# Where the operands of the projections lie: slots of 768 columns for tokens 258 to 1025, slots of 272 for the first 258

## The chip, the cores and the metric

The kernel runs on one core of one Trainium2 chip. A core has five engines that run side by side: TensorE (PE in the profile, with PEld for its weight loads) multiplies matrices, VectorE (DVE) and ScalarE (ACT) work elementwise, GpSimd (POOL) does a few of the subtractions here, and SyncE (SP) issues most of the DMAs. They share one on-chip memory of 128 partitions; matmul results go to eight banks of a second memory (PSUM), from which ACT and DVE take them away. The metric is the device time of one launch in microseconds (us); lower is better.

## The reference

One decoder layer in float32 over 16 meta tokens and 1024 tokens, model width 1024. The part that matters here:

```python
z = h @ w_in + b_in
q, k, v, c_in, gates = split(z)
a = swa_sink_attention(q, k, v, attn_sinks, rel_bias)      # 512 wide
y_attn = a @ w_attn_proj                                   # 512 -> 1024
c = c_val * sigmoid(c_gate)
c = causal_dwconv(c, conv_dw, conv_dw_b)                   # 31 taps
c = silu(layer_norm(c, conv_ln_g, conv_ln_b))              # 512 wide
y_conv = c @ w_conv_proj                                   # 512 -> 1024
mixed = sigmoid(g_attn) * y_attn + sigmoid(g_conv) * y_conv
h = layer_norm(alpha * h + mixed @ w_out, ln1_g, ln1_b)
```

A feed-forward network with a three-tap convolution follows (up, gelu, down) and a last layer norm. The output leaves out the meta tokens.

## The kernel before, in words

**Arithmetic.** Every float32 operand of a large product is split in two parts, hi (the value rounded to the matmul's float32r type) and lo (the rest). A product is three matmuls: weight hi by moving hi, weight hi by moving lo, weight lo by moving hi. `product` (lines 301, 305, 306) issues these three for each chunk of 128 of the contraction; the weights are the stationary operand (128 columns), the moving operand holds up to 512 tokens.

**Stages.** Layer norm and q, k, v come first; then attention runs beside the gate tiles (`ps_z`, 16 tiles of three column groups, 386, 384 and 256), which fill PE while ACT and DVE work on attention and on the depthwise convolution. While the last gate tiles run, DVE and ACT normalise the convolution (`cln_centre`, `cln_var`, `cln_rstd`, `cln_scale`, `cln_split`) and scale and split the attention output (`o_split`); means and variances come from small matmuls with a matrix of ones (`mean_mms`, lines 891 and 892, tile `ps_m`). Then come the projections (`ps_p`), the product with `w_out` (`ps_w`), FFN up (line 1497) and down (line 1635).

**Layout of the moving operands of the projections.** `OA` holds attention, `OC` the convolution, each [128, 8320] float32r: eight slots (four chunks of 128 channels, hi and lo of each) of T = 1040 columns, of which the last 1026 are tokens. `oo` and `conv` return the columns a to b of a slot.

**Groups of tokens.** `UG` cuts the 1026 tokens for the norm and the attention split: 386, 384, 256. `PG` cuts them for the projections: 258, 256, 256, 256.

**The projections.** The loop runs over eight tiles m of 128 output channels. `weights` loads the 128 columns of both projection matrices, [128, 8, 128], and splits them on ACT (cast to `whi`) and DVE or POOL (`wlo`, line 276). `whi` and `wlo` alternate between two buffers each; a `wlo` buffer is 64 columns longer than 1024, and `shift` says at which column of it the weights begin (16). Each m makes, for each of the four groups, 12 matmuls on `OA` and 12 on `OC`: 192 matmuls of 258 columns and 576 of 256 in all. `merge` multiplies the sums by the gates on DVE (lines 1097 to 1107).

**Order.** The tile framework's scheduler orders each engine's instructions by ranks and its own estimate of time; DVE's norm instructions are chained in the written order (`pin`). On each engine the instructions then run strictly in that order. The order of ACT in the norm's stretch, where evacuations of gate groups (line 676), casts of weights (273), squares, reciprocal roots (959) and swishes (971) alternate, is the scheduler's. A change of function on ACT costs a table load.

**Placement.** The pools give fixed addresses, the same before and after the change: `whi` at bytes 12224 and 16320 of a partition, `wlo` at 20416 and 24768, `OA` at 136896, `OC` at 196032.

Of the kernel before, what the change touches and what calls it, by code (L numbers as in the profile page):

```python
# [24 lines left out]
R = mybir.dt.float32r  # L25
# [4 lines left out]
P = 128  # L30
D = 1024
KC = D // P
NMETA = 16
S = 1024
T = S + NMETA
U0 = 14
# [16 lines left out]
ZG = [(0, 400), (400, 784), (784, 1040)]  # L53

HG = [(0, 272), (272, 656), (656, 1040)]
UG = [(0, 386), (386, 770), (770, 1026)]

PG = [(0, 258), (258, 514), (514, 770), (770, 1026)]

# [42 lines left out]
def tile_hybrid_layer(  # L102
# [9 lines left out]
    def load(o, i):  # L112
        return nc.sync.dma_start(out=o, in_=i)
# [5 lines left out]
    def f32(ap):  # L119
        return ap.bitcast(F)  # L120
# [6 lines left out]
    @contextmanager  # L127
    def rank(p):

        saved = tc.cur_priority  # L130
        tc.cur_priority = p
        yield
        tc.cur_priority = saved
# [34 lines left out]
    sp = start.enter_context(tc.tile_pool(name="start", bufs=1, side="right", reuse_waits="tile"))  # L168
# [93 lines left out]
    def wsp(name, tag):  # L262
        return wsp_p.tile([P, D + (64 if tag == "wlo" else 0)], R, name=name, tag=tag)

    def pair_of(hi, lo, shift=0, shape=None):
        hi, lo = wsp(hi, "whi"), wsp(lo, "wlo")[:, shift:shift + D]
        return [t.rearrange("p (k c) -> p k c", k=KC) for t in (hi, lo)] if shape else [hi, lo]

    def wraw(shape):
        return wraw_p.tile(shape, F, name="wr", tag="wr")  # L270

    def split(raw, hi, lo, quick=False, behind=None):
        ins = nc.scalar.copy(hi, raw)  # L273
        if behind is not None:
            after(ins, behind)
        return (nc.vector if quick else nc.gpsimd).tensor_tensor(lo, raw, f32(hi), OP.subtract)  # L276
# [1 line left out]
    fills = [0]  # L278
    last_fill, last_split = [], []

    def weights(shape, fill):
        fills[0] += 1
        n = fills[0]
        own = n == 3
        raw = sp.tile(shape, F, name="wr3") if own else wraw(shape)
        with rank({1: 13, 2: 18, 3: 17, 4: 23}.get(n, RK_SPLIT)):
            last_fill.append(fill(raw))
        hi, lo = (sp.tile(shape, R, name=t + "3") for t in ("whi", "wlo")) if own else pair_of("whi", "wlo", 16, shape)
        if n <= 3:
            return hi, lo, raw  # L290
        with rank(RK_SPLIT):
            last_split.append(split(raw, hi, lo, n <= 23))
        return hi, lo
# [3 lines left out]
    def product(ps, terms, behind=None):  # L297

        n = len(terms)
        for i, (ah, al, bh, bl) in enumerate(terms):  # L300
            ins = nc.tensor.matmul(ps, ah, bh, start=i == 0, stop=False)  # L301
            chunks_done.append(ins)
            if i == 0 and behind is not None:
                after(ins, behind)
            nc.tensor.matmul(ps, ah, bl, start=False, stop=False)  # L305
            last = nc.tensor.matmul(ps, al, bh, start=False, stop=i == n - 1)  # L306
        return last
# [404 lines left out]
    for q4 in range(2):  # L712
        ps = pat.tile([P, 512], F, name="ps_v4", tag="t", bufs=2)
        for i in range(4):
            c = NMETA + (q4 * 4 + i) * P
            nc.tensor.transpose(ps[:, i * P:(i + 1) * P], vT[:, c:c + P], ident)
        src = ps[:, :].rearrange("p (n g d) -> p n g d", g=2, d=HD)
        for g in range(NKV):
            hi, lo = (V[:, q4 * 4:q4 * 4 + 4, g, i] for i in range(2))
# [30 lines left out]
    for h in range(NH):  # L750
        g, r = divmod(h, 4)
        o = ps[:2, h * 16:(h + 1) * 16]
# [144 lines left out]
    with rank(RK_EVAC):  # L897
        nc.scalar.copy(c_hi[:, :U], csum)
        pinned.append(nc.vector.tensor_tensor(c_lo, csum, f32(c_hi[:, :U]), OP.subtract))
        for g, (a, b) in enumerate(UG):  # L900
            means[g] = pat.tile([P, 512], F, name="ps_m", tag="st"[g % 2], bufs=2)
# [7 lines left out]
    OC = late.tile([P, 8320], R, name="OC")  # L909
# [4 lines left out]
    OA = oa_p.tile([P, 8320], R, name="OA")  # L914
# [3 lines left out]
    def temp(n):  # L918
        return tmp_p.tile([P, 386], F, name="t", tag="t", bufs=6)[:, :n]


    def conv(c, hl, a, b):
        o = (c * 2 + hl) * T + U0
        return OC[:, o + a:o + b]

    def pin(ins):

# [7 lines left out]
    def cln_centre(g):  # L935
        a, b = UG[g]
        for c in range(CH):
            pin(dve.tensor_tensor(acc[c][:, a:b], acc[c][:, a:b], means[g][:, :b - a], OP.subtract))

    def cln_var(g):  # L940
        a, b = UG[g]
        n = b - a
        s_ = temp(n)
        nc.scalar.activation(s_, acc[0][:, a:b], AF.Square)
        for c in range(1, CH):
            q_ = temp(n)
            nc.scalar.activation(q_, acc[c][:, a:b], AF.Square)
            pin(dve.tensor_tensor(s_, s_, q_, OP.add))

        hi, lo = (conv(1, hl, a, b) for hl in range(2))  # L950
        pin(dve.tensor_copy(hi, s_))
        pin(dve.tensor_tensor(lo, s_, f32(hi), OP.subtract))
        sums[g] = pat.tile([P, 512], F, name="ps_m", tag="s", bufs=2)
        mean_mms(sums[g][:, :n], ones_r, hi, lo)

    def cln_rstd(g):
        n = UG[g][1] - UG[g][0]
        pv_, r_, t_ = sums[g][:, :n], temp(n), temp(n)
        nc.scalar.activation(r_, pv_, AF.Abs_reciprocal_sqrt, bias=eps, scale=1.0)
        pin(dve.scalar_tensor_tensor(t_, pv_, EPS, r_, OP.add, OP.mult))  # L960
        pin(dve.tensor_tensor(t_, t_, r_, OP.mult))
        pin(dve.tensor_scalar(t_, t_, -0.5, 1.5, OP.mult, OP.add))
        pin(dve.tensor_tensor(r_, r_, t_, OP.mult))
        rstd[g] = r_

    def cln_scale(g):
        a, b = UG[g]
        for c in range(CH):
            y = acc[c][:, a:b]
            pin(dve.tensor_tensor(y, y, rstd[g], OP.mult))  # L970
            nc.scalar.activation(y, y, AF.Silu, bias=clnb(c), scale=clng(c))

    def cln_split(g):
        a, b = UG[g]
        for c in range(CH):
            y = acc[c][:, a:b]
            pin(dve.tensor_copy(conv(c, 0, a, b), y))
            pin(dve.tensor_tensor(conv(c, 1, a, b), y, f32(conv(c, 0, a, b)), OP.subtract))


    def oo(r, hl, a, b):
        o = (r * 2 + hl) * T + U0
        return OA[:, o + a:o + b]

    def o_split(g, r):
        a, b = UG[g]
# [89 lines left out]
    tc.cur_priority = RK_PROJ  # L1076
    early = []
    for m in range(KC):
        hi, lo = weights([P, KC, P], lambda raw: load(raw, w_ab[m]))

        def branch(i, g, tag, bufs):
            a, b = PG[g]
            ps = pat.tile([P, 512], F, name="ps_p", tag=tag, bufs=bufs)
            rhs = (oo, conv)[i]
            product(ps[:, :b - a], [(hi[:, 4 * i + k], lo[:, 4 * i + k], rhs(k, 0, a, b), rhs(k, 1, a, b))
                                    for k in range(4)])
            return ps[:, :b - a]

        def merge(g, psa, psb):
            a, b = PG[g]  # L1090
            n = b - a
            with rank(RK_EVAC):
                t = gslot()[:, :, :n]
                ins = load(t, dram(sgd, m * P * U + a, [[U, P], [KC * P * U, 2], [1, n]]))

                ta, tb = t[:, 0], t[:, 1]
                nc.vector.scalar_tensor_tensor(ta, ta, 1.0, psa, OP.add, OP.mult)
                nc.vector.scalar_tensor_tensor(tb, tb, 1.0, psb, OP.add, OP.mult)
                nc.vector.tensor_tensor(ta, ta, tb, OP.add)
                if g == 0:  # L1100
                    nc.scalar.mul(pair[:, m, 0:2], ta[:, 0:2], 0.5)
                    nc.vector.scalar_tensor_tensor(pair[:, m, 2:4], ta[:, 0:2], 0.5, f32(pair[:, m, 0:2]),
                                                   OP.mult, OP.subtract)
                v = ta[:, n - 256:].rearrange("p (t x) -> p t x", t=2)
                h = mixed2(g, m, 0)
                last_act = nc.scalar.mul(h, v, 0.5)
                nc.vector.scalar_tensor_tensor(mixed2(g, m, 1), v, 0.5, f32(h), OP.mult, OP.subtract)
            return ins, last_act

        if m < KC - 1:  # L1110
            for g in range(4):
                last_gate, last_act = merge(g, branch(0, g, "mm", 3), branch(1, g, "t", 2))
        else:
            pa = [branch(0, g, "mm", 3) if g < 3 else branch(0, g, "s", 2) for g in range(4)]
            for g in range(4):
                last_gate, last_act = merge(g, pa[g], branch(1, g, "t", 2))
        if m in (2, 3):
            raw = (FA[:, 4112:5136], OB[:, 3072:4096])[m - 2]
            load(raw, w_out_v[m + 2])
            prep_wo(m + 2, raw, last_act)  # L1120
        if m < 4:
            early.append(FA[:, W_AT[m]:W_AT[m] + 1024])
            after(load(early[m], w_out_v[m]), last_gate)
# [349 lines left out]
    for c in range(FC):  # L1473
        V4, X, Z, Y = (pup.tile([P, 1024], F, name=n, tag=n) for n in ("pw", "px", "pz", "py"))
        passes = ((1,), (0,)) if c == 0 else ((0, 1),)
        for subs in passes:
            last = subs == passes[-1]
            w_next = iter(range(7))
            a, b = SUB[subs[0]][0], SUB[subs[-1]][1]
            i = max(a, 2)  # L1480
# [309 lines left out]
```

## Time and profile before

| | |
|---|---|
| median of 3 runs | 1259.55 us (1259.47 to 1259.66) |
| the profiled execution | 1259.33 us, of which the span of its instructions is 1257.1 us |
| PE busy | 1246.0 us (99%) |
| weight loads busy | 1179.2 us (94%) |
| DVE busy | 1086.6 us (86%) |
| ACT busy | 587.4 us (47%) |
| projections (first to last `ps_p`) | 416.48 to 512.07 us of the span |
| FFN up | about 609 to 1040 us |

How to read the rows: a row of the timeline holds the start (us from the span's start), the time of the instruction or of the merged group, the engine, the line, the operation, output tile <- input tiles, the shape and the count; in brackets idle time before it and what ended it. Matmuls overlap in the pipeline, so a matmul's own time is longer than the distance between two starts. PEclk is the clock that the throttle granted, in tenths.

### The profile page before, as it was taken

To read this page: it belongs to the slowest core of one execution; us is meant where nothing else is said; L and a number is where in the kernel's file an instruction comes from. 1 tells how busy PE (TensorE), PEld (TensorE's weight loads), DVE (VectorE), ACT (ScalarE), POOL (GpSimd) and SP (SyncE) were. 2 spreads that over 40 slices of the span, in tenths; PEclk is the share of its full clock that TensorE was granted. 3 is DMA by queue.
4 is the path that set the end of the run, shared out by engine and by line. 5 is a ranking of instruction groups with operands and counts; after the bars stand their busy time and mean duration, and the time that the engine had idled before them with its cause. 6 is when DMAs were issued, how large, how long until landed. Compare 5 with 4: busy or idle time off the path is not lost.

```text
span 1257.1 us, 21713 instructions
## 1 busy us (share of the span) xinstructions
PE 1246.0 (99%) x8546; PEld 1179.2 (94%) x8546; DVE 1086.6 (86%) x1859; ACT 587.4 (47%) x1057; POOL 54.1 (4%) x28
## 2 busy tenths in 40 slices
PE   9999999999999999999999999999999999999997
PEld 8999999999999999788899999999999998888886
DVE  7899989999989587648899999999999986995697
ACT  7522244545474222335565555554555554544330
POOL 0000000010112132000000000000000000000000
PEclk9999999999999999999999999999999999999999
DMA  7294733332155565222145555463464568998722
GB/s 279 73 309 104 192 95 97 106 94 81 68 141 178 155 171 140 77 75 101 68 134 185 193 210 187 184 218 117 154 230 164 203 211 318 390 328 298 249 86 84
DMA packets 96152, 212.10 MB, mean 169 GB/s; under 512 B 10787, under 2 KB 35939, under 8 KB 95922
## 3 DMA queue, kind: packets, MB, share of 16 engines
q1 hardware_dynamic: 84282, 199.64, 47.4%
q10 hardware_dynamic: 11768, 11.08, 2.7%
q8 instruction: 67, 1.10, 0.4%
q14 instruction: 35, 0.29, 0.1%
HBM read 150.29 MB, written 62.70 MB: 169 GB/s over the span
## 4 chain that ended last, share of the span: by engine, by line
PE 96%; ACT 1%; DVE 1%; DMA 0%; issue 0%; ACTq 0%; DVEq 0%; SPq 0%
PE px L1497 14%; PE py L1497 9%; PE ps_x L1635 9%; PE ps_z L305 8%; PE ps_z L301 8%; PE ps_z L306 8%; PE ps_z L1635 7%; PE pz L1497 5%; PE pw L1497 5%; PE ps_p L306 2%; PE ps_p L301 2%; PE ps_p L305 2%; PE ps_w L306 2%; PE ps_w L301 2%; PE ps_w L305 2%; PE ps_z L517 2%
## 5 line engine op out<-in xcount | busy, mean ns | idle before, releaser
L669 DVE SCALAR_TENSOR_TENSOR FA<-cin,cols,FA 128x1026 f32<-128x1026 f32 x120 | 155.2, 1305 | 0.2
L301 PE MATMUL ps_z<-RHO,whi 128*128 128x384 f32 (+2 forms) x324 | 104.7, 323 | 0.2 <-ACT FA L676 0.2
L305 PE MATMUL ps_z<-RHC,whi 128*128 128x384 f32 (+2 forms) x324 | 104.5, 323 | 0.0
L305 PE MATMUL ps_z<-RHO,whi 128*128 128x384 f32 (+2 forms) x324 | 104.0, 321 | 0.0
L306 PE MATMUL ps_z<-RHC,wlo 128*128 128x384 f32 (+2 forms) x324 | 103.7, 320 | 0.0
L301 PE MATMUL ps_z<-RHC,whi 128*128 128x384 f32 (+2 forms) x324 | 103.7, 320 | 0.0
L306 PE MATMUL ps_z<-RHO,wlo 128*128 128x384 f32 (+2 forms) x324 | 103.4, 319 | 0.0
L1316 DVE TENSOR_TENSOR RHO<-wr,RHO 128x512 fp32r<-128x512 f32 x94 | 63.6, 686 | 5.4 <-ACT RHO L1315 5.4
L1315 ACT CAST RHO<-wr 128x512 fp32r<-128x512 f32 x94 | 56.7, 620 | 24.4 <-DVE wr L1333 11.5
L273 ACT CAST whi<-wr 128x1024 fp32r<-128x1024 f32 x37 | 38.9, 1051 | 56.3 <-PE ps_z L305 31.9
L301 PEld LDWEIGHTS ps_z<-RHO,whi 128*128 128x128 f32 x324 | 60.9, 188 | 0.9 <-ACT FA L676 0.4
L305 PEld LDWEIGHTS ps_z<-RHC,whi 128*128 128x128 f32 x324 | 60.9, 188 | 0.4
L306 PEld LDWEIGHTS ps_z<-RHC,wlo 128*128 128x128 f32 x324 | 60.9, 188 | 0.2
L301 PEld LDWEIGHTS ps_z<-RHC,whi 128*128 128x128 f32 x324 | 60.9, 188 | 0.2
L306 PEld LDWEIGHTS ps_z<-RHO,wlo 128*128 128x128 f32 x324 | 61.0, 188 | 0.1
L305 PEld LDWEIGHTS ps_z<-RHO,whi 128*128 128x128 f32 x324 | 60.9, 188 | 0.1
L1333 DVE TENSOR_TENSOR wr<-wr 128x512 f32<-128x512 f32 x88 | 60.3, 685 | 0.2
L276 POOL TENSOR_TENSOR wlo<-wr,whi 128x1024 fp32r<-128x1024 f32 x17 | 42.3, 2488 | 185.3 <-ACT whi L273 175.7
L676 ACT ACTIVATE FA<-ps_z,cols 128x386 f32<-128x386 f32 (+2 forms) x48 | 26.0, 541 | 46.6 <-PE ps_z L306 39.1
L1509 ACT COPY FA<-px 128x514 f32<-128x514 f32 (+2 forms) x23 | 13.1, 571 | 68.0 <-PE px L1497 67.8
L1316 DVE TENSOR_TENSOR ws<-wr,ws 128x512 fp32r<-128x512 f32 x60 | 40.6, 686 | 4.5 <-ACT ws L1315 4.3
L1422 ACT ACTIVATE FA<-OB,cols 128x512 f32<-128x512 f32 x44 | 35.9, 816 | 14.0 <-DVE OB L1505 14.0
(467 smaller groups left out, 3567.3 us busy)
## 6 DMA issues: line engine op xcount, KB each, us to landing
wr<-in_w_up_dram SPq DMA_DIRECT2D x44, 512.0 KB, 4.6
wr<-in_w_z_dram SPq DMA_DIRECT2D x30, 512.0 KB, 4.0
fd<-FA SPq DMA_DIRECT2D x44, 256.0 KB, 2.5
OB<-in_w_down_dram SPq DMA_DIRECT2D x19, 512.0 KB, 6.2
qt<-qd SPq DMA_DIRECT2D x28, 256.0 KB, 3.7
td<-OB SPq DMA_DIRECT2D x12, 512.0 KB
sums<-fd SPq DMA_DIRECT2D x12, 512.0 KB, 4.8
sd<-sums SPq DMA_DIRECT2D x12, 512.0 KB, 2.7
```

The source lines that it names most:

```text
L273: ins = nc.scalar.copy(hi, raw)
L276: return (nc.vector if quick else nc.gpsimd).tensor_tensor(lo, raw, f32(hi), OP.subtract)
L301: ins = nc.tensor.matmul(ps, ah, bh, start=i == 0, stop=False)
L305: nc.tensor.matmul(ps, ah, bl, start=False, stop=False)
L306: last = nc.tensor.matmul(ps, al, bh, start=False, stop=i == n - 1)
L669: nc.vector.scalar_tensor_tensor(acc[c], cin[:, j:j + U], wc, acc[c], OP.mult, OP.add)
L1315: nc.scalar.copy(hi, src)
L1316: ins = nc.vector.tensor_tensor(lo, src, f32(hi), OP.subtract)
L1333: ins = nc.vector.tensor_tensor(*x)
L1422: nc.scalar.activation(t, cc[:, 2:HW], AF.Identity, bias=ffw(3, o), scale=ffw(2, o))
L1497: ins = nc.tensor.matmul(o, x[:, ks], bmat(sub, q, hl, k), start=first and k + j == 0, stop=k == 3 and j == 2, skip_group_check=not first)
L1635: nc.tensor.matmul(banks[i], l[:, ts], r[:, ws], start=first and a and x + k == 0, stop=z and x == len(ops) - 1 and k == 2, skip_group_che ...
```

## The change

The slots change their places: the first 258 tokens of each of the eight slots lie apart, in pieces of 272 columns at the beginning (slots 0 to 2) and at the end (slots 3 to 7) of `OA` and `OC`; the other 768 tokens of each slot lie in pieces of 768 columns between them. `UG` becomes 258, 384, 384, so that no group crosses the cut. The low weights of the projections begin at column 0 of their buffer instead of 16; other weights keep 16. Every matmul keeps its shape except the twelve for the means and variances of the norm. By the scheduler, some instructions on ACT and PE stand elsewhere around the norm and at the end of the projections.

```diff
-UG = [(0, 386), (386, 770), (770, 1026)]
+UG = [(0, 258), (258, 642), (642, 1026)]
...
-    def weights(shape, fill):
+    def weights(shape, fill, shift=16):
...
-        hi, lo = (sp.tile(shape, R, name=t + "3") for t in ("whi", "wlo")) if own else pair_of("whi", "wlo", 16, shape)
+        hi, lo = (sp.tile(shape, R, name=t + "3") for t in ("whi", "wlo")) if own else pair_of("whi", "wlo", shift, shape)
...
+    def place(i, a, b):
+
+        if a < 258:
+            o = i * 272 + (6144 if i > 2 else 0)
+        else:
+            o = 816 + i * 768 - 258
+        return slice(o + a, o + b)
+
     def conv(c, hl, a, b):
-        o = (c * 2 + hl) * T + U0
-        return OC[:, o + a:o + b]
+        return OC[:, place(c * 2 + hl, a, b)]
...
     def oo(r, hl, a, b):
-        o = (r * 2 + hl) * T + U0
-        return OA[:, o + a:o + b]
+        return OA[:, place(r * 2 + hl, a, b)]
...
-        hi, lo = weights([P, KC, P], lambda raw: load(raw, w_ab[m]))
+        hi, lo = weights([P, KC, P], lambda raw: load(raw, w_ab[m]), 0)
```

## The prediction

> **What bounds the kernel.** I read the page first (span, busy shares, the chain), then the stage of the projections by itself, then single starts on TensorE (PE).
>
> ```profile
> span 1257.1 us, 21713 instructions
> PE 1246.0 (99%) x8546; PEld 1179.2 (94%) x8546; DVE 1086.6 (86%) x1859; ACT 587.4 (47%) x1057; POOL 54.1 (4%) x28
> PEclk9999999999999999999999999999999999999999
> PE 96%; ACT 1%; DVE 1%; DMA 0%; issue 0%; ACTq 0%; DVEq 0%; SPq 0%
> ```
>
> PE is busy 99% of the span at full clock, and 96% of the chain that ended last is PE. So a nanosecond between two matmul starts is a nanosecond of the kernel, and work on the other engines counts only where it makes PE wait. The change touches the stage of the projections (tile `ps_p`). Its window, for the matmuls of that tile alone (columns: stretch, its length, then busy time and count on PE, on the weight loads and on DVE, clock, DMA):
>
> ```profile
> 416.48:512.07 95.59, 90.99 (x768) 90.94 (x768) 26.44 (x63) 1.00 0.48 134
> ```
>
> 768 matmuls in 90.99 us are 118.5 ns each. The timeline shows their starts (first column, us). One output tile is two runs of 12 with 258 columns and then six runs of 12 with 256:
>
> ```profile
> 439.20 0.28 PE L301 MATMUL ps_p<-OA,whi 128*128 128x258 f32 x1
> ...
> 442.07 0.28 PE L301 MATMUL ps_p<-OA,whi 128*128 128x256 f32 x1
> ...
> 450.55 0.28 PE L301 MATMUL ps_p<-OA,whi 128*128 128x258 f32 x1
> ```
>
> 24 matmuls of 258 columns take 442.07 - 439.20 = 2.87 us, 119.6 ns each; 72 of 256 take 8.48 us, 117.8 ns each. The third number of a row (0.28) is the modelled end of one matmul and not the spacing. Eight tiles of this make 8 x 11.35 = 90.8 us, the 90.99 of the window. Now the same shape in the next stage, FFN up (L1497), where a row holds a whole run of 12:
>
> ```profile
> 690.17 1.60 PE L1497 MATMUL px<-RHC,RHO 128*128 128x258 f32 x12
> 691.61 1.52 PE L1497 MATMUL px<-OC,RHO 128*128 128x256 f32 x12
> ...
> 702.78 1.52 PE L1497 MATMUL py<-OC,RHO 128*128 128x256 f32 x12
> 704.14 1.52 PE L1497 MATMUL px<-OA,RHO 128*128 128x256 f32 x12
> 705.50 1.52 PE L1497 MATMUL px<-RHC,RHO 128*128 128x256 f32 x12
> 706.86 1.52 PE L1497 MATMUL py<-OA,ws 128*128 128x256 f32 x12
> 708.22 1.52 PE L1497 MATMUL py<-RHC,ws 128*128 128x256 f32 x12
> 709.58 0.28 PE L1497 MATMUL px<-RHC,ws 128*128 128x258 f32 x1
> ```
>
> From 702.78 to 709.58 are 60 matmuls of 256 columns in 6.80 us: 113.3 ns, 4.5 ns under the projections, same clock, same order (high part twice, low part once). The run of 258 at 690.17 takes 1.44 us, 120.0 ns: two columns more cannot cost 6.7 ns where 256 cost 113.3 (0.44 each, so 0.9).
>
> **The distances.** What differs is where the operands lie. The pools put `whi` at bytes 12224 and 16320 of a partition, `wlo` at 20416 and 24768, `OA` at 136896 and `OC` at 196032: each leaves 192 when divided by 256. A chunk of weights is 512 bytes, which keeps the remainder. Before, a slot of the projections is 1040 columns, 4160 = 16 x 256 + 64 bytes, so from slot to slot the remainder moves on by 64, and `wlo` begins 16 columns later, at remainder 0. In up, the runs of 256 columns begin at column 48 or 2048 n + 48 of `OC`, `OA` or `RHC`, remainder 128, and step by 1024 bytes; their weights, hi and lo, are all at remainder 192: one distance, 113.3 ns. The runs of 258 step by 1032 bytes, so their distances wander: 120.0 ns. The modulus 256 is my reading of these runs; no row prints an address.
>
> After, tokens from 258 on lie in slots of 768 columns, 3072 = 12 x 256 bytes, beginning 816 columns into `OA` and `OC`: remainder 192 + 3264, that is 128. With shift 0 `wlo` is at 192 like `whi`. Every moving slice then lies 64 bytes from its weights, as in up's runs of 256: the three groups of 256 get the operand distance of the rows of 113.3 ns.
>
> **The sum, part by part.**
> 1. 576 matmuls of 256 columns (8 tiles x 72): from 117.8 to 113.4 (113.3 in the rows; I leave 0.1 for the joints with runs at other distances): -2.5 us, all on PE with nothing beside it. Bounds: 0 if the distance is not the cause, -2.6 at 113.3.
> 2. 192 matmuls of 258 columns (first tokens, slots of 272 columns, 1088 = 4 x 256 + 64 bytes): the distance still steps by 64. Lower bound, all at the good distance: 113.3 + 0.9 = 114.2, -1.0 us; upper bound the wandering 120.0 of row 690.17, +0.1, for the range +0.3, since no run shows these very steps. I take +0.1, the end nearest to what the slots still do.
> 3. Split by 258/384/384: as many instructions on ACT and DVE as before and 1026 columns in both; the mean and variance matmuls (L891, L892) likewise. Nothing on a queue of SP or POOL is added; two loads on SP change places.
> 4. The order on ACT moves, and there is one PE wait:
>
> ```profile
> 382.08 0.28 PE L306 MATMUL ps_z<-RHC,wlo 128*128 128x256 f32 x1
> 382.56 0.44 PE L301 MATMUL ps_z<-RHO,whi 128*128 128x386 f32 x1 [0.21 <-ACT FA L676]
> 382.84 0.34 PE L305 MATMUL ps_z<-RHO,whi 128*128 128x386 f32 x1
> 383.02 0.33 PE L306 MATMUL ps_z<-RHO,wlo 128*128 128x386 f32 x1
> ```
>
> ```profile
> 375.00 1.06 ACT L273 CAST whi<-wr 128x1024 fp32r<-128x1024 f32 x1 [0.76 <-ACT FA L676]
> 375.97 0.46 ACT L676 ACTIVATE FA<-ps_z,cols 128x256 f32<-128x256 f32 x1
> 376.45 1.28 ACT L959 ACT_TABLE_LOAD   x1
> 376.46 0.33 ACTq L117 DMA_DIRECT2D sgd<-FA  x1
> 377.74 0.47 ACT L959 ACTIVATE t<-ps_m,eps 128x256 f32<-128x256 f32 x1
> 378.23 1.28 ACT L971 ACT_TABLE_LOAD   x1
> 379.53 2.51 ACT L971 ACTIVATE FA<-FA,cols 128x384 f32<-128x384 f32 x4
> 381.94 0.56 ACT L676 ACTIVATE FA<-ps_z,cols 128x386 f32<-128x386 f32 x1
> ```
>
> PE starts a gate group at 382.56, 0.48 after the matmul before it instead of 0.12, and the next start is 0.28 later instead of 0.18: 0.46 us lost. The bank it wants is emptied by the ACT evacuation at 381.94. Behind the cast of 375.00 stand, before it, an evacuation, a table load, a reciprocal root, a table load and four swishes: 5.9 us from the cast's end. In the changed order the last reciprocal root stands ahead of the cast, and behind the cast come one table load (1.28), four swishes (2.51), one evacuation (0.46) and an issue (0.33), 4.6 us. With the cast's end no later than 376.0 the bank is free by 381.2, a microsecond before PE wants it (382.2). I take the whole wait out: -0.45; bounds -0.46 and +0.3 (the cast late by another table load and a root, 1.75: the bank is free at 382.95, and the wait grows to 0.75).
> 5. The third column group of the projections (514 to 770) now needs the last part of attention, which it did not need before:
>
> ```profile
> 411.99 0.43 DVE L991 TENSOR_TENSOR OA<-OB,OA 128x256 fp32r<-128x256 f32 x1
> ...
> 422.19 0.28 PE L301 MATMUL ps_p<-OA,whi 128*128 128x256 f32 x1
> ```
>
> DVE is done at 412.42 and that group begins at 422.19: 9.8 us of cover, so 0. If it were gone, each microsecond DVE is later is one of PE.
>
> Sum: -2.5 + 0.1 - 0.45 = -2.85. Behind the stage PE is the chain, and the engines that follow it start earlier by as much. The profiled execution took 1259.33 us (2.2 more than its span), 0.2 under the median 1259.55 of the runs: 1256.5 against it, 1256.7 against the median.
>
> **A rule that speaks against it.** The rows have one shape at 117.8 and at 113.3 ns. The Trainium skill, "TensorE: Matmul & The Clock Gate", Back-to-back issue gap, gives the warm gap of a single matmul by its column count alone (an estimate by it for 256 columns: 109.2 ns), and its Part 2 says that loading the next weights "doesn't steal SBUF read bandwidth from the running matmul". By that rule the addresses cannot matter and part 1 would be 0 instead of -2.5; this trace does not agree with one gap per shape.
>
> **Rivals.**
> - The distance is not the cause, and 4.5 ns belong to something else of the stage, for instance its three source lines or the writes of the merges beside it. Then only the wait goes: 1259.55 - 0.45 = 1259.1. For it: no row prints an address. Against it: up has both figures, 113.3 and 120.0, in one stage and from one line. Chance 0.12. The page's rule above would give this time.
> - The matmuls gain but the wait of 0.46 stays, moves or doubles, since ACT's order is another: 1259.55 - 2.4 = 1257.15, up to 1257.5 with +0.3. Chance 0.20.
> - Slower: PE is held in the norm itself. PE reaches the variance matmul of the first group one gate group earlier than now.
>
> ```profile
> 357.00 0.56 DVE L952 TENSOR_TENSOR OC<-t,OC 128x386 fp32r<-128x386 f32 x1
> ...
> 358.92 4.00 DVE L948 TENSOR_TENSOR t<-t 128x384 f32<-128x384 f32 x3
> ```
>
> ```profile
> 359.74 0.34 PE L891 MATMUL ps_m<-OC,ones_r 128*128 128x386 f32 x1
> ```
>
>   DVE has its operand at 357.56, 2.2 us before PE takes it. With 258 columns instead of 386 DVE gets there about 1.2 us earlier (an estimate: nine instructions, 0.56 for 386 in row 357.00 and 0.43 for 256 in row 411.99), and PE by the 12 matmuls of 256 that now stand behind, 1.4; some 2.0 are left. Row 358.92 shows three instructions in 4.00 us which take 1.9 undisturbed: 2.1 lost once. One such loss ahead of the matmul costs PE 0.1 us; three (6.3 - 2.0 = 4.3) outweigh the gain: 1259.55 - 2.85 + 4.3 = 1261.0. It decides from 4.9 us of delay on; the trace has one loss there. Chance 0.07.
>
> **How the numbers follow.** The likeliest case, 0.61, gives 1256.7, with a range of its own from 1255.6 (part 2 at -1.0) to 1257.3 (the wait half kept, part 2 at +0.3). The second rival reaches 1257.5 and the first 1259.1; to leave no more than 2 in 10 out the range goes from 1255.6 to 1258.4, where half a gain of part 1 would also lie. 0.2% is 2.5 us, about what a measurement of this kernel tells from no change: faster than 1257.03 means most of the likeliest case and a little of the second, 0.57; within 0.2% are the rest of these and the first rival, 0.36; slower 0.07.
>
> **What would show it.** Part 1: runs of 12 of 256 columns in `ps_p` take 1.36 us instead of 1.41. Part 2: those of 258 stay near 1.43. Part 4: no start on PE is marked as released by ACT L676 near 382. Part 5: no gap in PE at the third group of the first tile. The prediction is wrong if the runs of 256 stay at 1.41, or if a PE gap over 1 us stands between 355 and 425.

## The result, and the profile after

The changed kernel takes 1257.75 us (median of 22 runs, 1257.42 to 1258.00) against 1259.41 (22 runs) for the kernel before: ratio 0.9986, 95% interval 0.9980 to 0.9991. It is faster by 1.66 us, 0.13%: a real difference, since the interval lies below 1, but within the 0.2% that the forecast set as a bound, the outcome to which it gave 0.36. The forecast was 1256.7, 2.85 us less, with a range from 1255.6 to 1258.4; the time lies inside it, and the size was too large by 1.2 us. The profiled execution took 1257.53 us, 2.1 more than its span.

The page of the changed kernel (span, busy time of each engine, and the chain that ended last):

```profile
span 1255.4 us, 21714 instructions
PE 1244.7 (99%) x8546; PEld 1178.1 (94%) x8546; DVE 1086.2 (87%) x1859; ACT 586.4 (47%) x1057; POOL 54.0 (4%) x28
...
PE 97%; DVE 1%; ACT 1%; DMA 0%; issue 0%; SPq 0%; DVEq 0%
```

PE is still the whole chain. The span is 1.7 us shorter, and PE has 1.3 us less to do. In the window of the projections (stretch, length, then busy time and count on PE, on the weight loads and on DVE, clock, DMA) the same 768 matmuls take 89.90 instead of 90.99 us, at the same granted clock (summed from start to start it is 1.25 us less; the busy time also counts the modelled end of the last matmul of a stretch, and the changed kernel has one stretch more):

```profile
416.27:510.17 93.90, 89.90 (x768) 89.84 (x768) 26.44 (x63) 1.00 0.50 141
```

The starts on PE (timeline of the changed kernel) show where. A tile is 24 matmuls of 258 columns and 72 of 256; rows with 258 on `OA` begin a tile, the others are starts of runs of 12:

```profile
419.17 0.29 PE L301 MATMUL ps_p<-OA,whi 128*128 128x256 f32 x1
...
420.55 0.28 PE L301 MATMUL ps_p<-OC,whi 128*128 128x256 f32 x1
...
421.91 0.28 PE L301 MATMUL ps_p<-OA,whi 128*128 128x256 f32 x1
...
427.35 0.28 PE L301 MATMUL ps_p<-OA,whi 128*128 128x258 f32 x1
...
430.24 0.28 PE L301 MATMUL ps_p<-OA,whi 128*128 128x256 f32 x1
...
438.72 0.28 PE L301 MATMUL ps_p<-OA,whi 128*128 128x258 f32 x1
...
441.62 0.29 PE L301 MATMUL ps_p<-OA,whi 128*128 128x256 f32 x1
...
449.79 0.28 PE L301 MATMUL ps_p<-OA,whi 128*128 128x258 f32 x1
```

The tiles take turns. In tiles 0 and 2 the 72 matmuls of 256 columns take 427.35 - 419.17 = 8.18 and 449.79 - 441.62 = 8.17 us, with runs of 12 at 1.36 (420.55 to 421.91): 113.3 ns a matmul, as forecast. In tile 1 they take 438.72 - 430.24 = 8.48 us, 117.8 ns, as before the change. This goes on to the end: tiles 0, 2, 4 and 6 are short, 1, 3 and 5 long. The last tile, which has its own order, has both:

```profile
496.13 0.29 PE L301 MATMUL ps_p<-OA,whi 128*128 128x256 f32 x1
...
500.22 0.28 PE L301 MATMUL ps_p<-OC,whi 128*128 128x258 f32 x1
...
501.66 0.29 PE L301 MATMUL ps_p<-OC,whi 128*128 128x256 f32 x1
...
503.03 0.39 PE L301 MATMUL ps_w<-RX,RHC 128*128 128x512 f32 x1
...
508.77 0.28 PE L301 MATMUL ps_p<-OC,whi 128*128 128x256 f32 x1
...
510.18 0.39 PE L306 MATMUL ps_w<-OA,RHC 128*128 128x512 f32 x1
```

Its 36 on `OA` take 500.22 - 496.13 = 4.09 us, 113.6 each; its first 12 on `OC` take 1.37; then come matmuls of the next product, and the last run of 12 on `OC` takes 510.18 - 508.77 = 1.41 again. So one and the same set of weights and slots runs at both spacings.

The account in the profiled executions: the 576 matmuls of 256 columns take 1.42 us less (four tiles at 0.31, the last one 0.18), the 192 of 258 take 0.17 more (441.62 - 438.72 = 2.90 and 430.24 - 427.35 = 2.89 us for 24, against 2.87). The wait of PE at 382 is gone, which the first experiment shows, and the stage begins 0.21 us earlier (416.27 against 416.48). Both together are 1.46. Of the remaining 0.2 of the span, most lies in a wait at the beginning of FFN up. The rows before and after it, first of the kernel before, then of the changed one:

```profile
618.42 1.58 PE L1497 MATMUL px<-RHC,ws 128*128 128x256 f32 x12
619.83 1.58 PE L1497 MATMUL py<-RHC,ws 128*128 128x256 f32 x12
621.72 0.99 PE L1497 MATMUL px<-RHC,RHO 128*128 128x258 f32 x6 [0.31 <-ACT OB L1509]
```

```profile
616.92 1.52 PE L1503 MATMUL px<-RHC,ws 128*128 128x256 f32 x12
618.28 1.59 PE L1503 MATMUL py<-RHC,ws 128*128 128x256 f32 x12
619.98 1.69 PE L1503 MATMUL px<-RHC,RHO 128*128 128x258 f32 x12
```

From the start of the last run of 256 to the next are 1.89 us before and 1.70 after. This pause differs from kernel to kernel (in the runs below 0.30 to 0.91 us lie between the last start ahead of it and the first behind it), so a difference of some tenths between two kernels can come from there.

The rows ahead of the pause show something that the forecast overlooked. The run at 618.42 takes 619.83 - 618.42 = 1.41 us before, and the same run takes 618.28 - 616.92 = 1.36 us after, though the change touches neither the shapes nor the addresses of this stage. In the kernel before, five of the first seven runs of 256 in FFN up (609.05 to 619.83) take 1.41 to 1.42 us; the other two have a wait in or behind them, and every run from 629.24 on takes 1.36. So the stage that served as the model had both spacings, at one distance, before anything was changed.

**Two theories** stood after this. A, the buffer: `whi` and `wlo` alternate between two buffers, and the remainders of `wlo` by 512 differ (448 and 192), so that the weights of even tiles suit the slots and those of odd tiles do not. B, the state: at these distances two spacings hold themselves, 113.3 and 117.8 ns, and what ran just before (the 24 matmuls of 258 columns, whose distances still wander) sets the one or the other. The last tile speaks against A, but its order is its own.

### The profile page after: what moved, and what is told of

Read it like the earlier page. It is cut to its first block, busy times and chain, and to the rows that moved or that the text cites. A ratio compares the mean times of both kernels' runs of the same rounds, so it can differ in the third digit from the quotient of the medians.

```text
span 1255.4 us, 21714 instructions
## 1 busy us (share of the span) xinstructions
PE 1244.7 (99%) x8546; PEld 1178.1 (94%) x8546; DVE 1086.2 (87%) x1859; ACT 586.4 (47%) x1057; POOL 54.0 (4%) x28
## 4 chain that ended last, share of the span: by engine, by line
PE 97%; DVE 1%; ACT 1%; DMA 0%; issue 0%; SPq 0%; DVEq 0%
PE px L1503 15%; PE py L1503 9%; PE ps_x L1641 9%; PE ps_z L305 8%; PE ps_z L301 8%; PE ps_z L306 8%; PE ps_z L1641 7%; PE pz L1503 5%; PE pw L1503 5%; PE ps_p L301 2%; PE ps_p L306 2%; PE ps_p L305 2%; PE ps_w L306 2%; PE ps_w L301 2%; PE ps_w L305 2%; PE ps_z L517 2%
```

## The experiments

### The split of norm and attention alone

```diff
 (the kernel before)
-UG = [(0, 386), (386, 770), (770, 1026)]
+UG = [(0, 258), (258, 642), (642, 1026)]
```

> The kernel before with the split of norm and attention by 258, 384 and 384 tokens alone; slots and distances stay. Both theories on the spacing expect all runs of 12 matmuls of 256 columns at 1.41 us and those of 258 near 1.43. If the change's norm part is what took the wait of 0.46 us at 382 away, the wait is gone here too, the projections begin some 0.2 us earlier (as after the change) and the time is 0.2 to 0.5 us under before. If the wait went for another reason (the new places of the slots moved the scheduler's order), it stands here and the time is that of before.

Measured: 1259.32 us against 1259.65, ratio 0.9997 (0.9988 to 1.0007), which does not tell it from no change. Runs of 256 columns stay at 1.41 us. The wait is gone, by the same order on ACT as in the changed kernel (ACT's timeline of this kernel):

```profile
374.26 0.58 ACT L959 ACTIVATE t<-ps_m,eps 128x384 f32<-128x384 f32 x1
374.74 1.04 ACT L273 CAST whi<-wr 128x1024 fp32r<-128x1024 f32 x1
...
379.86 0.57 ACT L676 ACTIVATE FA<-ps_z,cols 128x386 f32<-128x386 f32 x1
```

The last reciprocal root stands ahead of the cast, the bank is empty at 380.43, and PE goes on without a pause. So the split alone takes the wait away. But the projections begin at 416.42, only 0.06 us earlier than before and not the expected 0.2. A gate matmul that starts at 342.06 in the kernel before, ahead of the norm, already starts 0.16 later in this one (342.21); the way from it to the projections is 0.22 shorter (74.20 instead of 74.42). That is still less than the wait was worth, and the rest is lost next to the wait; the rows are those of the kernel before and then of the changed one, which does the same:

```profile
342.06 0.42 PE L305 MATMUL ps_z<-RHC,whi 128*128 128x384 f32 x1
```

```profile
342.14 0.42 PE L305 MATMUL ps_z<-RHC,whi 128*128 128x384 f32 x1
...
382.24 0.28 PE L306 MATMUL ps_z<-RHC,wlo 128*128 128x256 f32 x1
382.35 0.34 PE L301 MATMUL ps_z<-RHO,whi 128*128 128x386 f32 x1
382.53 0.34 PE L305 MATMUL ps_z<-RHO,whi 128*128 128x386 f32 x1
```

From the row at 342 to the first matmul of the projections are 416.48 - 342.06 = 74.42 us before and 416.27 - 342.14 = 74.13 after: 0.29 less, where the wait was worth 0.47 (0.48 + 0.28 became 0.11 + 0.18). The other 0.18 goes back into the matmuls beside it: the stretch to the matmul ahead of the wait takes 40.10 instead of 40.02 us, and the rest of the way another 0.1. From start to start most of it, 0.13, lies in the 146 gate matmuls of 384 columns on this way (25.61 us instead of 25.48). The gate matmuls have the same shapes and addresses as before, but the small matmuls for the variance (258 and 384 columns instead of 386, 384 and 256) stand elsewhere among them. That these shift the spacing of their neighbours is argued from theory B, not shown. The figure is steady: in the twelve other kernels here the same way takes 74.13 to 74.20.

### Two distances again

```diff
 (the changed kernel)
-        hi, lo = weights([P, KC, P], lambda raw: load(raw, w_ab[m]), 0)
+        hi, lo = weights([P, KC, P], lambda raw: load(raw, w_ab[m]), 16)
```

> The changed kernel with the low weights back at column 16, so that high and low weights have two distances from the moving slices (remainders 192 and 0 by 256, moving slices 128). If the one distance is what brought the shorter spacing, no run of 256 columns takes 1.36 us and the projections' 1.4 us are lost: 0.3 us under before at most. If equal steps of the slots (768 columns) alone are the cause, runs of 1.36 us stay in the even tiles and the time is that of the changed kernel.

Measured: 1260.21 us, ratio 1.0003 (0.9994 to 1.0012). No run is short in any tile (begin of tile 0's runs of 256 and of tile 1, of this kernel):

```profile
419.44 0.28 PE L301 MATMUL ps_p<-OA,whi 128*128 128x256 f32 x1
...
427.95 0.28 PE L301 MATMUL ps_p<-OA,whi 128*128 128x258 f32 x1
```

72 of 256 columns take 8.51 us, 118.2 ns each. Slots in equal steps bring no gain without the low weights at the high ones' remainder: the place of the operands is a cause, and the first rival of the forecast falls.

### The buffers' roles swapped

```diff
 (the changed kernel)
-        hi, lo = weights([P, KC, P], lambda raw: load(raw, w_ab[m]), 0)
+        hi, lo = weights([P, KC, P], lambda raw: load(raw, w_ab[m]), 64)
```

> The changed kernel with the low weights at column 64: the remainder by 256 stays (192), by 512 the two buffers of the low weights change roles (448 and 192). Theory A, the buffer: a pair of high and low weights with one certain remainder by 512 is good; then the odd tiles take 1.36 us for a run of 12 with 256 columns and the even ones 1.41, the reverse of the changed kernel. Theory B, the state: at one distance two spacings hold themselves, and what runs before (the 24 matmuls of 258 columns) decides; then the tiles still alternate, and which ones are good does not follow the buffer: even ones at 1.36 again, if the entry is the same.

Measured: 1258.01 us, ratio 0.9986 (0.9977 to 0.9995). Tile 0's runs of 256 columns, then tile 1's:

```profile
419.90 0.29 PE L301 MATMUL ps_p<-OA,whi 128*128 128x256 f32 x1
...
428.08 0.28 PE L301 MATMUL ps_p<-OA,whi 128*128 128x258 f32 x1
...
430.97 0.28 PE L301 MATMUL ps_p<-OA,whi 128*128 128x256 f32 x1
...
439.45 0.28 PE L301 MATMUL ps_p<-OA,whi 128*128 128x258 f32 x1
```

8.18 and 8.48 us, and so on in every tile as in the changed kernel, though the remainders by 512 are swapped between the buffers. Theory A, put by these remainders, falls. A shift by 256 bytes changes nothing: here the modulus 256 of the forecast holds.

### Two tiles without a run of 258 between them

```diff
 (the changed kernel)
-            for g in range(4):
+            for g in ((0, 1, 2, 3), (1, 2, 3, 0))[m % 2]:
```

> The changed kernel with the token groups of every odd tile but the last in the order 256, 256, 256, 258, so that two tiles' runs of 256 columns follow each other with no run of 258 between. Theory A, the buffer: even tiles at 1.36 us for a run of 12, odd ones at 1.41, the time is that of the changed kernel. Theory B, the state: both tiles of a pair hold one spacing, since nothing between them changes it; pairs at 1.36 or 1.41 throughout, and the time is between 1.0 us less (all good) and 1.4 us more than the changed kernel.

Measured: 1257.02 us, ratio 0.9978 (0.9970 to 0.9987). Begin of tile 0's runs of 256, of tile 1's, of the runs of 258 of tiles 1 and 2 together, and of tile 2's runs of 256:

```profile
419.18 0.29 PE L301 MATMUL ps_p<-OA,whi 128*128 128x256 f32 x1
...
427.35 0.28 PE L301 MATMUL ps_p<-OA,whi 128*128 128x256 f32 x1
...
435.51 0.28 PE L301 MATMUL ps_p<-OA,whi 128*128 128x258 f32 x1
...
441.30 0.29 PE L301 MATMUL ps_p<-OA,whi 128*128 128x256 f32 x1
...
457.63 0.28 PE L301 MATMUL ps_p<-OA,whi 128*128 128x258 f32 x1
```

Tile 1 takes 435.51 - 427.35 = 8.16 us for its 72, 113.3 ns each, with the weights, slots and addresses that took 8.48 in the changed kernel. Only what came before differs, so the buffer does not decide by any other property either. That is theory B: the spacing is kept from run to run, and the runs of 258 turn it. After 48 of them in a row (435.51 to 441.30) the next 144 are at 113.4 (457.63 - 441.30 = 16.33); after 24 in a row the spacing has turned in the changed kernel, both ways.

### 24 taken apart into 12 and 12

```diff
 (the changed kernel)
-            for g in range(4):
-                last_gate, last_act = merge(g, branch(0, g, "mm", 3), branch(1, g, "t", 2))
+            first = branch(0, 0, "mm", 3)
+            for g in (1, 0, 2, 3):
+                psa = branch(0, g, "mm", 3) if g else first
+                last_gate, last_act = merge(g, psa, branch(1, g, "t", 2))
```

> The changed kernel with the 24 matmuls of 258 columns of a tile taken apart: 12 on OA, two runs of 256, then the 12 on OC, four runs of 256. In the changed kernel 24 of them in a row turned the spacing of the runs of 256 from the one to the other, and 12 in the last tile left it at 113.3. Theory B with this rule: no tile alternates; all tiles before the last hold the spacing that the first one enters with, at 113.3 in all (1.372 us for the run behind a run of 258 and 1.360 for the others; the 576 take 65.5 us instead of 66.4 and the time is 0.6 to 1.0 us under the changed kernel) or at 117.8 in all (67.8, and 1.4 us over the changed kernel). If the buffer or the tile's number decides, even tiles stay at 1.36 and odd ones at 1.41. If the turn has no such rule, tiles mix.

Measured: 1256.78 us against 1259.43, ratio 0.9980 (0.9971 to 0.9989). From tile 1 of this kernel, the first of the four runs of 256 behind the run of 258 on `OC`, and the begin of tile 2:

```profile
432.99 0.29 PE L301 MATMUL ps_p<-OA,whi 128*128 128x256 f32 x1
...
438.44 0.28 PE L301 MATMUL ps_p<-OA,whi 128*128 128x258 f32 x1
```

438.44 - 432.99 = 5.45 us for 48 matmuls of 256 columns are 113.5 ns, with runs of 1.372 behind a run of 258 and 1.360 otherwise. All tiles are like this; no tile alternates. The 576 take 65.6 us instead of 66.4 (and 67.8 before the change), as expected to 0.1. Only the last two runs on `OC`, behind the matmuls of the next product, are at 1.413. By its own comparison this kernel is 2.65 us under the kernel before, where the change gives 1.66; the alternating order above, at 2.63, is as fast as far as the intervals tell.

### Other values of the one distance

Moving minus weights, by 256 bytes, is 192 after the change (128 - 192; the forecast's "64 bytes from its weights" is this distance, counted the other way). With one, two or four slots of first tokens ahead of the others instead of three it is 64, 128 and 0; the runs of 258 keep their distances. The diff for 64; for the other two, 272 and 0 become 544 and 1, and 1088 and 3:

```diff
 (the changed kernel)
-            o = i * 272 + (6144 if i > 2 else 0)
+            o = i * 272 + (6144 if i > 0 else 0)
...
-            o = 816 + i * 768 - 258
+            o = 272 + i * 768 - 258
```

> The changed kernel with one slot of the first tokens ahead of the slots of 768 columns instead of three, so that these begin at column 272 and not 816: still one distance for all, but another (moving slices at remainder 0 by 256, weights at 192). The 258 columns' distances stay as they are. Theory B as it stands (equal distance is what counts, the runs of 258 set the state) expects the picture of the changed kernel: even tiles 1.36 us for 12 of 256, odd ones 1.41, time within 0.3 us of the changed kernel. If the value of the distance counts too, the runs take another time, or all tiles one of the two.

> The changed kernel with two slots of first tokens ahead: slots of 768 from column 544, one distance of 128 bytes (moving minus weights, by 256). By the three distances measured so far (192: 113.3 or 117.8 ns, 64: 117.8 in this layout, 0: 120.0) each distance has spacings of its own. If only 192 can be fast, as in FFN up, the runs of 12 take 1.41 or more in every tile and the time is 1259 or above; if 128 is at least as far from a collision as 192, some or all take 1.36.

> The same with four slots ahead: the slots of 768 begin at column 1088, moving slices at remainder 192, like the weights: distance 0. Theory B as it stands expects again 1.36 and 1.41 by turns. If distance 0 means that weights and moving slices collide, all runs of 256 take 1.41 or more, the 1.4 us of the change are lost and the time is about that of before.

Measured: distance 64, 1259.35 us (0.9997, 0.9987 to 1.0007); distance 128, 1260.24 (1.0002, 0.9992 to 1.0013); distance 0, 1260.80 (1.0011, 1.0000 to 1.0021). In each all tiles are alike. Begin and end of 72 matmuls of 256 columns, for 64, for 128 and for 0:

```profile
431.62 0.28 PE L301 MATMUL ps_p<-OA,whi 128*128 128x256 f32 x1
...
440.10 0.28 PE L301 MATMUL ps_p<-OA,whi 128*128 128x258 f32 x1
```

```profile
419.22 0.29 PE L301 MATMUL ps_p<-OA,whi 128*128 128x256 f32 x1
...
427.77 0.28 PE L301 MATMUL ps_p<-OA,whi 128*128 128x258 f32 x1
```

```profile
430.78 0.29 PE L301 MATMUL ps_p<-OA,whi 128*128 128x256 f32 x1
...
439.42 0.28 PE L301 MATMUL ps_p<-OA,whi 128*128 128x258 f32 x1
```

8.48, 8.55 and 8.64 us: 117.8, 118.8 and 120.0 ns. One distance for all is not enough; its value counts, and of the four only 192 has a spacing of 113.3. With distance 64, 128 or 0 no gain is shown: all three intervals reach 1, and at 0 the whole interval lies at or above it.

### One distance for the runs of 258 too

Here weights and slots both move on by 64 bytes from chunk to chunk, so that slots of 1040 columns, next to each other as before, have one distance for each group. For room, the norm's temporaries have five buffers; PE has no wait from that (74.18 to 74.20 us for the way from 342 to the projections).

```diff
 (the changed kernel)
-            o = i * 272 + (6144 if i > 2 else 0)
...
+        o = (hl * 4 + k) * T + U0
...
-        hi, lo = weights([P, KC, P], lambda raw: load(raw, w_ab[m]), 0)
+        hi, lo = (wsp(n, n).rearrange("p (c z) -> p c z", c=4)[:, :, 0:256].rearrange(
+            "p c (h x) -> p c h x", h=2) for n in ("whi", "wlo"))
...
-            product(ps[:, :b - a], [(hi[:, 4 * i + k], lo[:, 4 * i + k], rhs(k, 0, a, b), rhs(k, 1, a, b))
+            product(ps[:, :b - a], [(hi[:, k, i], lo[:, k, i], rhs(k, 0, a, b), rhs(k, 1, a, b))
```

The second has 16:272 for 0:256, the third (k + 2) % 4 for k in the slot, the fourth is the third with the alternating order of groups.

> One distance for the runs of 258 too, which the changed kernel left uneven: slots of 1040 columns as before, but the four high parts first and then the four low ones, and the weights of the chunks 272 columns apart, so that weights and slots move on by the same 64 bytes: 256 columns at distance 64, 258 at 56 (moving minus weights, by 256). The pool of temporaries in the norm has five instead of six buffers, for room. Theory B: nothing changes the state inside the stage, so all eight tiles hold one spacing, and the runs of 258 take 1.37 us (114.2 ns each) or 1.42; in the good case the projections take 87.3 us, 3.2 less than after the change gave up to before (90.99), and the time is some 2 us under the changed kernel, in the bad one all runs of 256 take 1.41 and the time is near that of before. If only the width of 258 is what makes those runs long, they stay at 1.43 or more.

> The same with the weights 16 columns on: 256 columns at distance 0, 258 at 248. Theory B expects one spacing for the whole stage, as for the kernel with distances 64 and 56; which of the two spacings it enters with may differ. If distance 0 collides, all runs are at 1.41 or longer.

> The kernel whose weights and slots move on by the same 64 bytes, with the slots turned by two places (chunk k at place k + 2 by four), so that the distance is 192 for 256 columns, as after the change and in FFN up, and 184 for 258. The value of the distance decides the spacing: 113.3 for the runs of 256 in all tiles, 1.36 us, since no run of 258 at wandering distances stands between; 65.3 us for the 576 of them, 1.1 under the changed kernel. The 258 columns at 1.37 if the wandering made them long, near 1.44 (as at distance 56) if their width or this distance does. Time: 1256.5 to 1257.0, or 1255.5 with short runs of 258. If two spacings stand at 192 whatever precedes, tiles at 1.41 turn up here too and the time is at 1257.5 or above.

> The same with the group of 258 columns last in every odd tile but the last, so that half as many joints between 258 and 256 stand in the stage. A joint costs 25 ns in the run behind it (1.391 against 1.366 at distance 64): three or four joints fewer are 0.1 us, no more than the measurement can tell from the kernel with distance 192 in the plain order. It shows whether the state holds when four runs of 258 follow each other.

Measured: distance 64, 1257.39 us (0.9982, 0.9973 to 0.9992); distance 0, 1259.32 (0.9998, 0.9988 to 1.0007); distance 192, 1259.18 (0.9996, 0.9987 to 1.0005); the same in alternating order, 1259.21 (0.9996, 0.9987 to 1.0005). Rows of the kernels with 64, with 0 and with 192:

```profile
428.21 0.28 PE L301 MATMUL ps_p<-OA,whi 128*128 128x258 f32 x1
...
431.08 0.28 PE L301 MATMUL ps_p<-OA,whi 128*128 128x256 f32 x1
...
439.31 0.28 PE L301 MATMUL ps_p<-OA,whi 128*128 128x258 f32 x1
```

```profile
430.69 0.28 PE L301 MATMUL ps_p<-OA,whi 128*128 128x256 f32 x1
...
439.28 0.28 PE L301 MATMUL ps_p<-OA,whi 128*128 128x258 f32 x1
...
442.13 0.28 PE L301 MATMUL ps_p<-OA,whi 128*128 128x256 f32 x1
...
450.49 0.28 PE L301 MATMUL ps_p<-OA,whi 128*128 128x258 f32 x1
```

```profile
430.51 0.29 PE L301 MATMUL ps_p<-OA,whi 128*128 128x256 f32 x1
...
438.94 0.28 PE L301 MATMUL ps_p<-OA,whi 128*128 128x258 f32 x1
```

My expectation of these failed where I was surest. With distance 192, the one of the changed kernel and of FFN up, the 72 take 8.43 us in every tile, 117.1 ns, and the alternating order changes nothing in that; with distance 64, which gave 117.8 before, they take 8.23, 114.3 in the mean and 1.366 us for a run of 12 behind the first. With distance 0 the stage begins at 8.59 (119.3) and goes over to 8.36 (116.1) from the third tile on; the last tile, behind a single run of 258, begins at 119.4 again (496.86 to 501.16 for 36). Here too one set of addresses has two spacings, and here the longer one comes back behind 12 matmuls of 258 columns. So the distance of a slice from its own weights does not decide the spacing either. What these kernels change beside it is that the remainder moves by 64 from chunk to chunk, so that the next matmul's weights, which are loaded while a slice streams, lie at another distance from that slice (the loads run beside the matmuls: 89.84 us of them in the 89.90 us of the window). After the change that second distance, next weights minus slice, is always 64; with 192 in the pitched layout it is 64 for two matmuls of three and 128 for the third. That it is the cause is a guess; it does not by itself give the figures above (next weights at 192 are 117.8 in one layout, and at 192 and 0 by turns 113.9 in the other).

The runs of 258 columns take 2.87 us for 24 (431.08 - 428.21), as before the change, although their distances no longer wander. So the wandering was not what makes them long; whether it is their width or these distances (56, 248, 184) is open.

## Why the prediction was right, and where it was wrong

The time lay in the range and the sign was right, but 1.08 us of the 2.5 of the main term did not come. 1257.75 lies above the likeliest case's own range (1255.6 to 1257.3); it is inside the whole range because that was widened for rivals that did not come. The forecast's own sign of being wrong, runs of 256 that stay at 1.41, came in three of eight tiles. Point by point:

1. **576 matmuls of 256 columns, -2.5 us forecast, -1.42 measured.** This is the term that failed. The step was: "Every moving slice then lies 64 bytes from its weights, as in up's runs of 256: the three groups of 256 get the operand distance of the rows of 113.3 ns." Every slice did get that distance, and 113.3 is what the even tiles run at; but the distance does not fix the spacing. At the same addresses 117.8 holds itself as well, and the 24 matmuls of 258 columns between two tiles turn the one into the other. Four tiles gained 0.31 us each, three nothing, the last one 0.18. The rows that the forecast took from FFN up show one spacing; the first runs of the same stage, in the same profile, show the other. With the 24 taken apart the term measured 65.59 - 67.84 = -2.25; of what is missing, 0.2 are the runs behind a run of 258 (1.372 for 1.360, sixteen times), for which I had left 0.1 ns a matmul or 0.06 us, and 0.1 are the two last runs.
2. **192 matmuls of 258 columns, +0.1 forecast, +0.17 measured**, inside the bounds. The lower bound, 114.2 ns at a good distance, was not reached by any layout.
3. **The new split, 0:** it added no instruction on PE, DVE, ACT or POOL (the counts of the page are as before) and no wait of its own. Whether the 0.18 us in point 4 belong here is not settled.
4. **The wait at 382, -0.45 forecast.** It went, by the path that the forecast named: root ahead of the cast, bank empty at 380.4 (forecast: by 381.2). Worth on the way to the projections: -0.29 (-0.22 to -0.29 in the other kernels), since the matmuls around it spread by 0.18. I had taken a wait on PE for time that comes back whole.
5. **The third column group, 0:** it begins at 421.91, and no start is late. DVE's last instruction for `OA` ends at 413.14: 8.8 us of cover are left of the 9.8.

The forecast's own sum misses 1.08 us in point 1, 0.16 in point 4 and 0.07 in point 2: 2.85 - 1.08 - 0.16 - 0.07 = 1.54. Two things that it did not have make the rest: the row at 342 comes 0.08 later (342.14 against 342.06), and 0.2 are gained behind the projections, most of it in the shorter wait at the start of FFN up, which is luck, since that wait differs from kernel to kernel. 1.54 - 0.08 + 0.2 = 1.66, as in the medians.

**The rivals.** "The distance is not the cause" falls by the kernel with two distances (118.2 ns in all tiles) and by the four values of one distance. The Trainium skill, "TensorE: Matmul & The Clock Gate", Part 2, says that loading the next weights "doesn't steal SBUF read bandwidth from the running matmul"; the runs do not test its two read ports, but a spacing that follows from the shape alone, as in the gap formula for a single matmul of that page's Back-to-back issue gap, does not agree with 113.3 to 120.0 ns for one shape at one clock. "The matmuls gain but the wait stays" did not come. PE held in the norm did not come either: DVE had the operand of the first variance matmul at 356.44 and PE took it at 358.39, 1.95 us later, where the forecast put 2.0.

What was not among the rivals is the one that came: half a gain, since one layout has two stable spacings. The forecast names "half a gain of part 1" as a time that its range covers, without a mechanism for it.

## What to carry to other kernels

When PE is the chain, compare the spacing of starts for one shape across the kernel's stages: here the places of the operands in memory, and the order of the runs, are worth up to 6% of a matmul. A layout copied from a fast stage is a candidate and no promise; measure the spacing of every run in both stages, from the first on, not the mean of the stage or one stretch of it, and look whether it changes between runs of the same addresses. Where it does, try another order of the odd-shaped runs (here 12 and 12 instead of 24) before another layout.

## What was unexpected of the hardware

- One shape (128 x 256 columns, weights 128 x 128) at full granted clock ran at 113.3, 113.9, 116.1, 117.1, 117.8, 118.8, 119.3 and 120.0 ns, by the operands' places and by what ran before.
- At one and the same set of addresses two spacings hold themselves for dozens of matmuls: 113.3 and 117.8 (144 in a row at 113.4 in the kernel with alternating order, 72 at 117.8 in the odd tiles). In this layout 24 matmuls of 258 columns turned the one into the other, 12 did not, and after 48 it was the same as before them. That is no general rule: with distance 0 in the pitched layout 116.1 became 119.4 behind 12 of them, and in the changed kernel's last tile 113.3 became 117.8 behind matmuls of 512 columns.
- A shift of the low weights by 256 bytes left every run as it was to 2 ns in 1400; a shift by 64 bytes cost the whole gain.
- Open: which relation of addresses sets the spacing. The distance of a slice from its own weights does not (117.1 and 113.3 at 192, 117.8 and 113.9 at 64). A layout in which the runs of 258 too lie in steps that keep one remainder for weights and slots alike, as the runs of 256 do, needs 1.3 KB more for each of `OA` and `OC` and was not tried.
